# Hybrid decoder block: how the low parts of the mixers' and gates' weights are formed

## The chip, the cores and the metric

The kernel runs on one core of a Trainium2 chip. The metric is the device time of one execution in microseconds (us); the median of three runs of the kernel before is 965.05 us (963.51 to 967.03).

## The reference, cut to what matters

```python
u    = rmsnorm(h, norm1_g)
proj = u @ w_in            # split into q, k, v, z, decays (GDN), q, k, v, indexer (DSA), two gates
o_gdn = gated_delta_rule_chunked(...)   # after a causal conv of width 4 and SiLU on q, k, v
o_dsa = dsa_sparse_attention(...)       # top 128 keys by the indexer's score, then softmax
mixed = sigmoid(gate_a + ...) * o_gdn + sigmoid(gate_b + ...) * o_dsa
h = h + mixed @ w_out
h = h + (silu(gate) * val) @ ffn_w_down  # gate, val: a conv of width 3 over rmsnorm(h) @ ffn_w_up
out = rmsnorm(h)
```

The sequence has 512 tokens of 1024 channels, the gated delta net (GDN) 8 heads of 128, the sparse attention (DSA) 8 heads over 2 key and value heads, the feed-forward part 2816 channels. All of it is float32.

## The kernel before, in words

**Split products.** TensorE multiplies in a format (float32r, `R` in the code) that holds fewer bits than float32. So every large matrix product is made of three: each operand is split into a high part, the value rounded to that format, and a low part, what is left, rounded in its turn. `passes` (L198 to L204) adds high x low (L202), low x high (L203) and high x high (L204) into one accumulator in PSUM.

**Pieces.** The weights lie in DRAM as 139 pieces of 128 x 1024 values (512 KB). `load` (L184) takes three buffers from a pool, for the piece as it is (`raw`), its high part (`whi`) and its low part (`wlo`), three of each in turn, and issues the load on SyncE's queue (SP). `piece` (L192) lets ScalarE (`A`) cast `raw` into the high part (L194), and GpSimd (`P`) or VectorE (`V`) subtract that from `raw` into the low part (L195). The first three pieces, for the DSA values and the small columns, are loaded and split apart from that, in halves (`split`, L231 to L234).

**Who uses pieces.** `channel_major` (L304) takes two pieces for 256 output channels over all 512 tokens: 24 matmuls of 512 columns for each piece, into two accumulator banks. `token_major` (L292) takes two for 256 channels with tokens as rows: 48 matmuls of 256 columns for each. There are three accumulator banks of that kind (`acc`). In the order of the program:

- four pieces for the indexer's queries (L423), 12 for the first half of the GDN heads (`gdn_half(0)`), two for the DSA keys, eight for the DSA queries (L701), 12 for the second half (`gdn_half(1)`): all by `channel_major`;
- 24 for z and the two gates by `token_major` (`z_chunk`, `ga_chunk`, `gb_chunk`);
- then 8 for the output projection (L842), 44 for the FFN's up projection (L914) and 22 for the down projection (L961), each with its `piece` call.

In the first 62, GpSimd makes the low parts, but for six in `gdn_half(1)`, where VectorE makes that of the second piece of each pair. After them VectorE makes them, but for the first four of the up projection, which GpSimd makes.

**What runs beside.** For each GDN half, the accumulators go through a causal conv (`conv_silu`, taps on VectorE at L460), heads are transposed for their norms (L488, squares on ScalarE at L490), decays are masked by GpSimd (`affine_select`, L524) and exponentiated by ScalarE, GpSimd scales the queries (L542), and a triangular system is solved on blocks of 32: the blocks go to DRAM and come back (L568, L572), VectorE eliminates column by column (a product at L583, a subtraction at L585, 30 times), and the results go the same way back (L587, L589). These transfers are issued on ScalarE's queue. The indexer's top 128 of each row are found by VectorE (L688, L689). The attention (L705 to L732) is computed in items of a head and 128 queries: VectorE adds the mask and takes the maximum, ScalarE takes the exponential (L716), TensorE transposes (L724) and multiplies (L728).

**What sets the order.** The program is written in sequence, and a scheduler interleaves it when it is built: it plans the times of all instructions on a model and lays down a fixed order for each engine. Each engine then runs its own list in order and waits on semaphores; a transfer is issued by the engine whose queue it is on, in the order of that engine's list. The tile pool adds the waits for a buffer's last users.

```python
    def piece(lo_engine):
        raw, hi, lo = load()
        A.copy(hi, raw)
        lo_engine.tensor_sub(lo, raw, hi.bitcast(F))
        return hi, lo
```

Of the kernel before, what the change touches and what calls it, by code (L numbers as in the profile page):

```python
# [9 lines left out]
F = mybir.dt.float32  # L10
R = mybir.dt.float32r
I32 = mybir.dt.int32
AF = mybir.ActivationFunctionType
OP = mybir.AluOpType
# [72 lines left out]
def hybrid_block(ctx: ExitStack, tc: tile.TileContext, x: bass.AP, xc: bass.AP, wp: bass.AP,  # L87
                 chan: bass.AP, rows: bass.AP, out: bass.AP):
    nc = tc.nc
    V, A, P, T = nc.vector, nc.scalar, nc.gpsimd, nc.tensor  # L90
# [5 lines left out]
    def acc(name="acc"):  # L96
        return psum.tile([128, 512], F, name=name, tag="acc", bufs=3)

    def tp(name="tp"):
        return psum.tile([128, 512], F, name=name, tag="tp", bufs=2)  # L100
# [4 lines left out]
    def rec(name="rec"):  # L105
        return psum.tile([128, 512], F, name=name, tag="rec", bufs=2)
# [73 lines left out]
    pipe = ctx.enter_context(tc.tile_pool(name="pipe", bufs=1))  # L180
    pipe.tile([128, 16], F, name="pad1")
    pos = [0]

    def load():  # L184
        raw = pipe.tile([128, 1024], F, name="raw", bufs=3)
        nc.sync.dma_start(raw, wp[pos[0]])
        pos[0] += 1
        hi = pipe.tile([128, 1024], R, name="whi", bufs=3)
        lo = pipe.tile([128, 1024], R, name="wlo", bufs=3)
        return raw, hi, lo  # L190

    def piece(lo_engine):  # L192
        raw, hi, lo = load()
        A.copy(hi, raw)  # L194
        lo_engine.tensor_sub(lo, raw, hi.bitcast(F))  # L195
        return hi, lo

    def passes(o, lhs, rhs, first, last, shared=False):  # L198


        (lh, ll), (rh, rl) = lhs, rhs
        a = T.matmul(o, lh, rl, start=first, stop=False, skip_group_check=shared)  # L202
        T.matmul(o, ll, rh, start=False, stop=False, skip_group_check=shared)  # L203
        return a, T.matmul(o, lh, rh, start=False, stop=last, skip_group_check=shared)  # L204

    def cols(pc, k, n, c0, c1):
        return tuple(w.rearrange("p (k c) -> p k c", c=n)[:, k, c0:c1] for w in pc)
# [12 lines left out]
    xg = [tuple(sl.tile([128, S], R, name=n, bufs=KT) for n in ("xgh", "xgl")) for _ in range(KT)]  # L220
# [68 lines left out]
    def u_blk(k, tb):  # L289
        return uTh[:, k, 128 * tb:128 * tb + 128], uTl[:, k, 128 * tb:128 * tb + 128]  # L290

    def token_major(eng):  # L292

        pcs = [piece(eng), piece(eng)]
        ps = [acc().rearrange("p (t c) -> p t c", c=256) for _ in range(2)]
        for i in range(2):
            for tb in range(NT):
                for k in range(4):
                    kk = 4 * i + k
                    passes(ps[tb // 2][:, tb % 2], u_blk(kk, tb), cols(pcs[i], k, 256, 0, 256),  # L300
                           kk == 0 and tb % 2 == 0, kk == KT - 1, shared=True)
        return ps

    def channel_major(eng, src=None, second=P):  # L304
        pcs = [piece(eng), piece(second)]
        ps = [acc(), acc()]
        for i, pc in enumerate(pcs):
            for t in range(2):
                for k in range(4):
                    kk = 4 * i + k  # L310
                    passes(ps[t], cols(pc, k, 256, 128 * t, 128 * t + 128),
                           src[kk] if src else (uTh[:, kk], uTl[:, kk]), kk == 0, kk == KT - 1)
        return ps
# [4 lines left out]
    def half_kb(name):  # L318
        return PR.tile([128, 512], F, name=name, tag="dqo", bufs=9)
# [100 lines left out]

    iq = []
    for j in range(2):
        for t, p in enumerate(channel_major(P, xg)):  # L423
            iqf = PR.tile([128, 512], F, name="iqf", tag="t", bufs=5)
            V.tensor_mul(iqf, p, rB)  # L425
            for s in range(2):
                q = PR.tile([128, 512], R, name="iq", tag="dqo", bufs=9)
                src = iqf[64 * s:64 * s + 64]
                A.copy(q[0:64], src)
                V.tensor_sub(q[64:128], src, q[0:64].bitcast(F))  # L430
                iq.append(q)
# [6 lines left out]
    for b in range(1, NT):  # L438
        n = 128 * (b + 1)
        score[b] = mask[:, m_off[b]:m_off[b] + n]  # L440
        for h in range(H):
            p = tp("rel")[:, :n]
            T.matmul(p, iq[h][:, 128 * b:128 * b + 128], ikh[:, :n], start=True, stop=False)
            T.matmul(p, iq[h][:, 128 * b:128 * b + 128], ikl[:, :n], start=False, stop=True)
            w = iw[:, b, h:h + 1]
# [23 lines left out]
    def gdn_half(hh):  # L469
# [23 lines left out]


        for j in range(2):
            for t, p in enumerate(channel_major(P, second=V if hh else P)):
                conv_silu(p, 8 + HH * hh + 2 * j + t, kT[:, 2 * j + t])
        sumsq(kT, ssk, kt)
        V.tensor_scalar(ssk, ssk, EPS, None, op0=OP.add)
# [7 lines left out]
        V.tensor_mul(kd, rk, kde[:, :, hs])  # L507

        for j in range(2):
            for t, p in enumerate(channel_major(P, second=V if hh else P)):  # L510
                conv_silu(p, HH * hh + 2 * j + t, qT[:, 2 * j + t])
        sumsq(qT, ssq, None)
        V.tensor_scalar(ssq, ssq, EPS, None, op0=OP.add)
# [5 lines left out]
        for c in range(NT):  # L519
# [10 lines left out]
            for h2 in range(2):  # L530
                p = rec("kk").rearrange("p (h a i) -> p h a i", h=2, a=2)
# [13 lines left out]


        for j in range(2):
            for t, p in enumerate(channel_major(P, second=V if hh else P)):
                h = 2 * j + t
                vT = conv_silu(p, 16 + HH * hh + h)  # L550
                pv = rec("vt").rearrange("p (c d) -> p c d", d=128)
                for c in range(NT):
                    T.transpose(pv[:, c], vT[:, 128 * c:128 * c + 128], ident)
                for c in range(NT):
                    A.activation(vt[:, c, h], pv[:, c], AF.Identity, scale=nk[:, c, h:h + 1])
# [24 lines left out]
        for j in range(1, 31):  # L580
            m, c = 31 - j, (j + 1) // 2
            w = tw[:, :c * m].rearrange("p (r i) -> p r i", i=m)
# [93 lines left out]
        oA.append(at)  # L676

    gdn_half(0)


# [10 lines left out]


    dk = PR.tile([128, 2, 512], F, name="dk", tag="k4", bufs=2)
    for t, p in enumerate(channel_major(P)):
        A.copy(dk[:, t], p)
    dq = []
    for j in range(4):
        for t, p in enumerate(channel_major(P)):
            q = half_kb("dq")
            A.copy(q, p)  # L700
            dq.append(q)  # L701

    gdn_half(1)

    oB = []  # L705
# [60 lines left out]
        V.scalar_tensor_tensor(o, t, 1.0, o, op0=OP.add, op1=OP.mult)  # L766

    def z_chunk(j):
        for t2, p in enumerate(token_major(P)):
            t = tmp("tz")  # L770
            A.activation(t, p, AF.Tanh, scale=0.5)
            V.scalar_tensor_tensor(t, t, 1.0, p, op0=OP.add, op1=OP.mult)
            o = oAv[j][:, 2 * t2:2 * t2 + 2]
            P.tensor_mul(o, o, t)

    def ga_chunk(j):
        bias = gate_bias(256 * j)
        for t2, p in enumerate(token_major(P)):
            gated(oAv[j][:, 2 * t2:2 * t2 + 2], p, bias)

    def gb_chunk(j):
        bias = gate_bias(1024 + 256 * j)
        for t2, p in enumerate(token_major(P)):
            tb = slice(2 * t2, 2 * t2 + 2)
            t = tmp("tg")
            V.tensor_add(t, p, bias)
            A.activation(t, t, AF.Tanh, scale=0.5)
            for i in range(2):
                o = oB[2 * j + i][:, tb]
                V.scalar_tensor_tensor(o, t[:, :, 128 * i:128 * i + 128], 1.0, o, op0=OP.add, op1=OP.mult)  # L790
# [50 lines left out]
    for j in range(4):  # L841
        pcs = [piece(V), piece(V)]  # L842
# [70 lines left out]
    for f in range(NF):  # L913
        e = P if f < 2 else V  # L914
        pcs = [piece(e), piece(e)]
# [123 lines left out]
```

## Time and profile before

| what | value |
|---|---|
| median of three runs | 965.05 us |
| the profiled execution | 965.41 us |
| its span, first to last instruction | 963.4 us |
| mean granted TensorE clock | 0.990 |
| TensorE busy | 923.5 us |
| VectorE busy | 615.2 us |
| ScalarE busy | 439.7 us |
| GpSimd busy | 205.3 us |
| read from HBM | 85.18 MB |

The profile is of one execution; its span leaves out about 2 us around the first and the last instruction. Engines stand in it as PE (TensorE; PEld is its loading of weights), DVE (VectorE), ACT (ScalarE), POOL (GpSimd) and SP (SyncE); a q behind the name is the engine's queue of issues. Issuing a transfer is not counted as busy time. A line such as L195 is the kernel's. A group is written as what is written <- what is read, with the shape, the count, the busy time and the mean of one, then the idle time of the engine before these instructions and what ended it. PEclk is the granted clock, 1.00 for 2.4 GHz; the DMA share is that of the 16 engines' time. Matmuls are pipelined, so that the busy time of TensorE counts their overlap once.

### The profile page before, as it was taken

Reading aid. Unit: us, or ns where it says so; the run is one execution under the profiler, and the core shown is the slowest. Engines: PE = TensorE matmul, PEld = TensorE weight load, DVE = VectorE, ACT = ScalarE, POOL = GpSimd, SP = SyncE. Lnnn points to the kernel's source line nnn. Section 1 sums busy time; section 2 is a strip of 40 time slices with the busy share of each in tenths; the row PEclk is TensorE's granted clock in tenths of the full one; section 3 lists DMA queues with packets and bytes.
Section 4 is the critical chain, followed back from the end, with each engine's and each line's share of the span. In section 5 each row is a group of like instructions: output and inputs, shape, how many; then the busy total and the mean of one; then the engine's idle time right before and its main releaser. Section 6 shows DMA issues by size and latency. Waiting matters only on the chain.

```text
span 963.4 us, 14652 instructions
## 1 busy us (share of the span) xinstructions
PE 923.5 (96%) x5671; PEld 806.4 (84%) x5671; DVE 615.2 (64%) x1262; ACT 439.7 (46%) x938; POOL 205.3 (21%) x120
## 2 busy tenths in 40 slices
PE   8889998989999898899999999999999999999997
PEld 8768887767787797899999999888888888888886
DVE  5997999897638948755543637556655666522424
ACT  7436673422458653345544436444444444421313
POOL 2744343520211254211154022100000000000201
PEclk9999999998999999999999999999999999999999
DMA  8222222324310122311322223323232332323212
GB/s 322 93 87 88 88 72 83 100 65 110 111 45 25 64 77 85 98 55 50 137 72 91 85 90 97 100 87 102 96 104 94 88 110 87 110 90 107 88 66 87
DMA packets 39541, 89.29 MB, mean 93 GB/s; under 512 B 15632, under 2 KB 16944, under 8 KB 39472
## 3 DMA queue, kind: packets, MB, share of 16 engines
q1 hardware_dynamic: 24048, 82.05, 26.0%
q10 hardware_dynamic: 15424, 6.31, 2.7%
q8 instruction: 44, 0.72, 0.3%
q14 instruction: 25, 0.20, 0.1%
HBM read 85.18 MB, written 3.16 MB: 92 GB/s over the span
## 4 chain that ended last, share of the span: by engine, by line
PE 66%; DVE 22%; DMA 5%; ACT 3%; issue 2%; POOL 1%; ACTq 0%; SPq 0%; DVEq 0%; POOLq 0%
PE acc L202 17%; PE acc L204 17%; PE acc L203 17%; PE d L202 3%; PE d L203 3%; PE d L204 3%; DVE y L460 3%; DVE wi L585 2%; DVE mask L689 2%; DVE tw L583 2%; DVE top L688 2%; PE lg L728 1%; PE lg L710 1%; DMA ge<-gdr 1%; DMA nn<-bl 1%
## 5 line engine op out<-in xcount | busy, mean ns | idle before, releaser
L194 ACT CAST whi<-raw 128x1024 fp32r<-128x1024 f32 x136 | 142.3, 1047 | 175.7 <-PE acc L204 77.0
L195 POOL TENSOR_TENSOR wlo<-raw,whi 128x1024 fp32r<-128x1024 f32 x60 | 147.5, 2460 | 295.4 <-ACT whi L194 248.2
L195 DVE TENSOR_TENSOR wlo<-raw,whi 128x1024 fp32r<-128x1024 f32 x76 | 94.3, 1241 | 147.5 <-ACT whi L194 147.4
L203 PE MATMUL acc<-hTh,wlo 128*128 128x512 f32 (+1 forms) x368 | 139.8, 380 | 0.0
L202 PE MATMUL acc<-hTl,whi 128*128 128x512 f32 (+1 forms) x368 | 139.1, 381 | 0.2 <-DVE hTl L837 0.2
L204 PE MATMUL acc<-hTh,whi 128*128 128x512 f32 (+1 forms) x368 | 138.8, 380 | 0.0
L202 PE MATMUL acc<-uTl,whi 128*128 128x512 f32 x272 | 109.1, 402 | 5.3 <-DVE iqf L425 4.3
L203 PE MATMUL acc<-uTh,wlo 128*128 128x512 f32 x272 | 108.9, 400 | 5.1 <-DVE wlo L195 5.1
L204 PE MATMUL acc<-whi,uTh 128*128 128x256 f32 x384 | 113.3, 295 | 0.0
L202 PE MATMUL acc<-wlo,uTh 128*128 128x256 f32 x384 | 112.2, 292 | 0.0
L203 PE MATMUL acc<-whi,uTl 128*128 128x256 f32 x384 | 112.1, 292 | 0.0
L204 PE MATMUL acc<-uTh,whi 128*128 128x512 f32 x272 | 108.9, 400 | 0.0
L979 POOL TENSOR_TENSOR h<-h,gf 128x512 f32<-128x512 f32 (+1 forms) x8 | 10.6, 1344 | 338.6 <-ACT sq L975 338.6
L896 DVE SCALAR_TENSOR_TENSOR fy<-acc,ch,fy 128x511 f32<-128x511 f32 x88 | 65.8, 748 | 26.2 <-ACT fy L894 24.7
L202 PEld LDWEIGHTS acc<-hTl,whi 128*128 128x128 f32 x368 | 69.2, 188 | 13.5 <-DVE hTl L837 0.4
L204 PEld LDWEIGHTS acc<-hTh,whi 128*128 128x128 f32 x368 | 69.2, 188 | 13.1
L203 PEld LDWEIGHTS acc<-hTh,wlo 128*128 128x128 f32 x368 | 69.2, 188 | 13.1
L202 PEld LDWEIGHTS acc<-wlo,uTh 128*128 128x128 f32 x384 | 73.9, 193 | 1.6 <-issue 1.0
L204 PEld LDWEIGHTS acc<-whi,uTh 128*128 128x128 f32 x384 | 73.8, 192 | 1.7 <-issue 1.0
L203 PEld LDWEIGHTS acc<-whi,uTl 128*128 128x128 f32 x384 | 74.0, 193 | 1.2 <-issue 1.0
L202 PEld LDWEIGHTS acc<-uTl,whi 128*128 128x128 f32 x272 | 52.1, 192 | 16.6 <-DVE iqf L425 4.8
L203 PEld LDWEIGHTS acc<-uTh,wlo 128*128 128x128 f32 x272 | 52.1, 191 | 15.5 <-DVE wlo L195 5.5
(313 smaller groups left out, 1916.9 us busy)
## 6 DMA issues: line engine op xcount, KB each, us to landing
raw<-in_wp_dram SPq DMA_DIRECT2D x139, 512.0 KB, 3.4
xT<-in_xc_dram SPq DMA_DIRECT2D x8, 256.0 KB, 6.0
xt<-in_x_dram SPq DMA_DIRECT2D x4, 512.0 KB, 7.8
ge<-gdr ACTq DMA_DIRECT2D x8, 256.0 KB, 3.4
h<-in_x_dram SPq DMA_DIRECT2D x4, 512.0 KB, 6.0
out_dram<-h SPq DMA_DIRECT2D x8, 256.0 KB, 2.2
gbias<-in_rows_dram ACTq DMA_DIRECT2D x8, 128.0 KB, 3.1
nn<-bl ACTq DMA_DIRECT2D x4, 256.0 KB, 4.8
```

Source lines behind the costliest of these rows:

```text
L194: A.copy(hi, raw)
L195: lo_engine.tensor_sub(lo, raw, hi.bitcast(F))
L202: a = T.matmul(o, lh, rl, start=first, stop=False, skip_group_check=shared)
L203: T.matmul(o, ll, rh, start=False, stop=False, skip_group_check=shared)
L204: return a, T.matmul(o, lh, rh, start=False, stop=last, skip_group_check=shared)
L460: V.scalar_tensor_tensor(y[:, s:], p[:, :512 - s], cw[:, ti, 3 - s:4 - s], y[:, s:], op0=OP.mult, op1=OP.add)
L583: V.tensor_mul(w, wi[:, 0:c, j:j + 1].to_broadcast([128, c, m]), nn[:, j:j + 1, j + 1:].to_broadcast([128, c, m]))
L585: V.tensor_sub(wi[:, 0:c, j + 1:], wi[:, 0:c, j + 1:], w)
L688: V.max(top, score[b])
L689: V.match_replace(score[b], top, score[b], TAKEN)
L896: V.scalar_tensor_tensor(y[:, s:], p[:, :512 - s], fw[:, ti, 2 - s:3 - s], y[:, s:], op0=OP.mult, op1=OP.add)
L979: P.tensor_mul(hv, hv, gf[:, 512 * half + c.start:512 * half + c.stop])
```

## The change

In `piece`, a call that names no engine now does the following: ScalarE writes the negated piece, rounded, into the low part's buffer; a transfer issued by GpSimd then reads the piece from DRAM a second time and adds it to what stands there; ScalarE casts the high part after that. All calls from `channel_major` and `token_major` (62 pieces) name none, so GpSimd subtracts nothing there, and neither does VectorE in the second half. The output projection and the FFN call as before. For all pieces there are two buffers for `raw` instead of three, and four for `wlo` instead of three. Cut to one call of each kind:

```diff
     def load():
-        raw = pipe.tile([128, 1024], F, name="raw", bufs=3)
+        raw = pipe.tile([128, 1024], F, name="raw", bufs=2)
         nc.sync.dma_start(raw, wp[pos[0]])
         pos[0] += 1
         hi = pipe.tile([128, 1024], R, name="whi", bufs=3)
-        lo = pipe.tile([128, 1024], R, name="wlo", bufs=3)
+        lo = pipe.tile([128, 1024], R, name="wlo", bufs=4)
         return raw, hi, lo
 
-    def piece(lo_engine):
+    def piece(lo_engine=None):
+        w = wp[pos[0]]
         raw, hi, lo = load()
-        A.copy(hi, raw)
-        lo_engine.tensor_sub(lo, raw, hi.bitcast(F))
+        if lo_engine is None:
+            A.activation(lo, raw, AF.Copy, scale=-1.0)
+            P.dma_start(lo, w, accum_op=OP.add)
+            A.copy(hi, raw)
+        else:
+            A.copy(hi, raw)
+            lo_engine.tensor_sub(lo, raw, hi.bitcast(F))
         return hi, lo
...
-    def token_major(eng):
+    def token_major():
-        pcs = [piece(eng), piece(eng)]
+        pcs = [piece(), piece()]
...
-    def channel_major(eng, src=None, second=P):
-        pcs = [piece(eng), piece(second)]
+    def channel_major(src=None):
+        pcs = [piece(), piece()]
...
-            for t, p in enumerate(channel_major(P, second=V if hh else P)):
+            for t, p in enumerate(channel_major()):
```

## Rows read from the trace of the kernel before

**Rows 1.** The head of the page: the span, and each engine's busy time.

```profile
span 963.4 us, 14652 instructions
PE 923.5 (96%) x5671; PEld 806.4 (84%) x5671; DVE 615.2 (64%) x1262; ACT 439.7 (46%) x938; POOL 205.3 (21%) x120
```

**Rows 2.** Ten stages of the span, busy times in us, columns above them.

```profile
core 0: us, PE busy (x) PEld busy (x) DVE busy (x) ACT busy (x) POOL busy (x), PEclk, DMA share, GB/s
0.00:25.00 25.00, 21.96 (x146) 20.77 (x147) 13.74 (x36) 18.63 (x32) 6.85 (x14) 1.00 0.85 315
25.00:55.00 30.00, 27.42 (x120) 22.27 (x118) 29.21 (x41) 12.66 (x20) 20.20 (x10) 0.94 0.27 88
55.00:65.00 10.00, 5.41 (x18) 3.90 (x16) 9.72 (x34) 4.17 (x7) 3.75 (x2) 0.83 0.17 52
65.00:150.00 85.00, 84.87 (x413) 71.08 (x414) 77.50 (x173) 54.27 (x152) 33.06 (x17) 1.00 0.27 88
150.00:212.00 62.00, 58.73 (x281) 47.75 (x280) 58.70 (x143) 24.06 (x48) 28.18 (x17) 1.00 0.31 90
212.00:232.00 20.00, 14.48 (x50) 11.03 (x49) 15.03 (x46) 1.74 (x2) 0.00 (x0) 0.83 0.39 99
232.00:310.00 78.00, 74.06 (x594) 62.06 (x595) 49.56 (x99) 46.99 (x130) 11.97 (x7) 1.00 0.19 57
310.00:420.00 110.00, 99.92 (x896) 92.50 (x895) 82.80 (x228) 54.47 (x163) 39.66 (x24) 0.98 0.27 78
420.00:600.00 180.00, 179.98 (x1503) 176.37 (x1502) 96.81 (x229) 86.89 (x207) 48.65 (x23) 1.00 0.27 88
600.00:963.00 363.00, 356.68 (x1663) 298.75 (x1661) 182.17 (x238) 135.85 (x183) 12.99 (x9) 1.00 0.29 95
```

**Rows 3.** What TensorE waited for: us in total, times, longest us.

```profile
PE pT L724 <- ACT pe L716: 5.6, 4, 2.4
PE acc L203 <- DVE wlo L195: 5.1, 1, 5.1
PE acc L202 <- DVE iqf L425: 4.3, 1, 4.3
```

**Rows 4.** Page, line groups: low and high parts' casts and subtractions.

```profile
L195 POOL TENSOR_TENSOR wlo<-raw,whi 128x1024 fp32r<-128x1024 f32 x60 | 147.5, 2460 | 295.4 <-ACT whi L194 248.2
L194 ACT CAST whi<-raw 128x1024 fp32r<-128x1024 f32 x136 | 142.3, 1047 | 175.7 <-PE acc L204 77.0
```

**Rows 5.** Timeline of VectorE: start us, us, engine line, operation, tiles.

```profile
54.16 2.25 DVE L389 TENSOR_TENSOR gd<-gd,s 128x32 f32<-128x32 f32 x1
...
209.21 2.34 DVE L583 TENSOR_TENSOR tw<-wi,nn 128x105 f32<-128x105 f32 x1
...
211.88 0.28 DVE L583 TENSOR_TENSOR tw<-wi,nn 128x120 f32<-128x120 f32 x1
...
216.25 1.22 DVE L195 TENSOR_TENSOR wlo<-raw,whi 128x1024 fp32r<-128x1024 f32 x1
...
226.63 2.32 DVE L460 SCALAR_TENSOR_TENSOR y<-acc,cw,y 128x511 f32<-128x511 f32 x3 [0.51 <-ACT y L458]
...
380.41 2.47 DVE L585 TENSOR_TENSOR wi<-wi,tw 128x120 f32<-128x120 f32 x1
```

**Rows 6.** Timeline of GpSimd, 205 to 222 us, same columns.

```profile
208.43 2.99 POOL L195 TENSOR_TENSOR wlo<-raw,whi 128x1024 fp32r<-128x1024 f32 x1 [8.48 <-ACT whi L194]
```

**Rows 7.** Timeline of ScalarE and its queue, 196 to 240 us, same columns.

```profile
201.43 1.05 ACT L194 CAST whi<-raw 128x1024 fp32r<-128x1024 f32 x1 [3.95 <-issue]
...
224.56 1.30 ACTq L587 DMA_DIRECT2D bl<-wi  x2
```

**Rows 8.** DMA issues: tiles, queue, count, KB each, us to landing.

```profile
raw<-in_wp_dram SPq DMA_DIRECT2D x139, 512.0 KB, 3.4
...
nn<-bl ACTq DMA_DIRECT2D x4, 256.0 KB, 4.8
```

**Rows 9.** Line group of ScalarE's casts between 150 and 420 us.

```profile
L194 ACT CAST whi<-raw 128x1024 fp32r<-128x1024 f32 x31 | 32.5, 1047 | 25.9 <-issue 5.3 <-PE vt L553 4.9 <-POOL wlo L195 4.0
```

More of the change, by code (lines that the diff above doesn't have):

```diff
@@ L422, in hybrid_block @@
     for j in range(2):
-        for t, p in enumerate(channel_major(P, xg)):
+        for t, p in enumerate(channel_major(xg)):
             iqf = PR.tile([128, 512], F, name="iqf", tag="t", bufs=5)
@@ L509, in gdn_half @@
         for j in range(2):
-            for t, p in enumerate(channel_major(P, second=V if hh else P)):
+            for t, p in enumerate(channel_major()):
                 conv_silu(p, HH * hh + 2 * j + t, qT[:, 2 * j + t])
@@ L547, in gdn_half @@
         for j in range(2):
-            for t, p in enumerate(channel_major(P, second=V if hh else P)):
+            for t, p in enumerate(channel_major()):
                 h = 2 * j + t
@@ L693, in hybrid_block @@
     dk = PR.tile([128, 2, 512], F, name="dk", tag="k4", bufs=2)
-    for t, p in enumerate(channel_major(P)):
+    for t, p in enumerate(channel_major()):
         A.copy(dk[:, t], p)
@@ L697, in hybrid_block @@
     for j in range(4):
-        for t, p in enumerate(channel_major(P)):
+        for t, p in enumerate(channel_major()):
             q = half_kb("dq")
@@ L768, in z_chunk @@
     def z_chunk(j):
-        for t2, p in enumerate(token_major(P)):
+        for t2, p in enumerate(token_major()):
             t = tmp("tz")
@@ L777, in ga_chunk @@
         bias = gate_bias(256 * j)
-        for t2, p in enumerate(token_major(P)):
+        for t2, p in enumerate(token_major()):
             gated(oAv[j][:, 2 * t2:2 * t2 + 2], p, bias)
@@ L782, in gb_chunk @@
         bias = gate_bias(1024 + 256 * j)
-        for t2, p in enumerate(token_major(P)):
+        for t2, p in enumerate(token_major()):
             tb = slice(2 * t2, 2 * t2 + 2)
```

## The prediction

> **What bounds the kernel now.** I read the head of the page first, then the span by stages, what TensorE waits for, and last the timelines of the other engines in the stages where TensorE idles. TensorE is busy for 923.5 of 963.4 us [rows 1]: whatever the change does elsewhere, it can gain only out of the 40 us in which TensorE idles, and a little where its clock was held down. The stages say where those are [rows 2]. From 65 to 150 us and from 420 to 600 TensorE has no gap; after 600 the change touches only the number of buffers. What is left: 2.6 us idle in 25 to 55, 4.6 in 55 to 65, 3.3 in 150 to 212, 5.5 in 212 to 232, 3.9 in 232 to 310 and 10.1 in 310 to 420. In 55 to 65 and in 212 to 232 the granted clock is 0.83 besides, part of the time at 1.2 instead of 2.4 GHz after the idle time: 0.17 x 10 = 1.7 and 0.17 x 20 = 3.4 us more.
>
> In those stages VectorE is the late one: busy 29.2 of 30 us, then 9.7 of 10, then 58.7 of 62 [rows 2]. Two of the three longest waits of TensorE are on it: 5.1 us for a low part that VectorE itself writes, 4.3 us for an emptied accumulator (iqf) [rows 3]. And VectorE is late in part because of GpSimd. While GpSimd's subtraction ran from 208.43 to 211.42 [rows 6], a VectorE product of 105 columns took 2.34 us; the next one of its line, larger at 120 columns, took 0.28 [rows 5]. So a VectorE instruction stands until the subtraction is through. In the first half's triangular solve there are five such (at 181.77, 189.29, 192.51, 197.90 and 209.21 us, 1.6 to 2.2 us too long each, some 9.6 together; the last stands in the rows), in the second half three (near 373.7, 380.4 and 388.3, some 2 each; the middle one stands), and three between 37 and 57 us (7 together; 54.16 is the last) [rows 5].
>
> **What goes.** 56 of GpSimd's 60 subtractions at 2.46 us [rows 4], 138 us of GpSimd, and six of VectorE's at 1.22 [rows 5]. GpSimd's own time is on no path; the VectorE time that it held is. By stage, as share of TensorE's idle and slow-clock time: in 55 to 65, 5 of 6.3 us come back, since VectorE is 7 us earlier and TensorE's 4.3 us wait for it ends. In 25 to 55 nothing: the same relief is there, but the first low part now comes by a transfer instead of a 2.46 us subtraction, and TensorE waits for that. In 150 to 212, 1 us of 3.3. In 212 to 232, 6 of 8.9: the high part that TensorE needs was ready at 202.48 [rows 7], its low part stood in VectorE's order behind the solve until 216.25 [rows 5]; that wait of 5.1 us is gone. Late next are the accumulators: the conv taps that empty them stand behind the solve at 226.63 [rows 5], and with 9.6 + 1.2 us less ahead of them they come about when TensorE wants the banks. In 232 to 310, 1 us. In 310 to 420, 3 of 10.1: VectorE's solve there is 6 us shorter, but TensorE's longest wait is on ScalarE (5.6 us) [rows 3]. Sum: 5 + 1 + 6 + 1 + 3 = 16 us.
>
> **What comes on ScalarE.** 62 negating passes over 128x1024; the cast of that shape takes 1.05 us [rows 4], so 65 us. From 65 to 150 and 420 to 600 ScalarE has room (54.3 of 85, 86.9 of 180) and TensorE's queue of pieces covers it. In 310 to 420 the exponentials that TensorE waits for share ScalarE with some twelve passes; if a quarter of them stand in that chain, 12 x 1.05 / 4 = 3 us. Without cover, all of them: 12.6 us.
>
> **What comes as transfers.** 62 accumulating ones of 512 KB, issued by GpSimd behind the wait for ScalarE. No row shows one. Issue: between 0.65 us (an issue on ScalarE's queue, two in 1.30 [rows 7]) and 2.46, one pass of GpSimd over the data [rows 4]; I take 1, nearer the issue, as no element passes through the engine. What stands behind it on GpSimd (masks, qT, the z products) waited for 2.46 us before, so nothing gets later there. Landing: at least the plain load's 3.4 us [rows 8], at most three times that, 10.2, if the read of the source, the read of the old value and the write take turns; I take 6.8, since write and read overlap in the plain load too. The Trainium skill (Collectives: The Full Stack, "Why ReduceScatter is half of AllGather") says that an adding transfer is slower for its two source reads and not for the adding; by it the landing would be the same 6.8, as an estimate, and no run here shows it yet.
>
> Lead: a piece lasts 85 us x 88 GB/s = 7.5 MB, 14.3 pieces in 65 to 150, so 5.9 us [rows 2]. A high part waits for the buffer of three pieces back (the cast's idle time is ended by TensorE [rows 4]) and so is ready two pieces, 11.8 us, early. The low part has four buffers and may start three pieces early, 17.7 us. It needs 1.05 + 1 + 6.8 = 8.9 us, at the upper ends 1.05 + 2.46 + 10.2 = 13.7. Hidden at either end, so nothing in the steady stages.
>
> The four small transfers in each half's solve (nn<-bl, 4.8 us [rows 8], and three others) share the engines with twice the bytes: between 0 and half of 4.8 each; I take 0.4 x 8 = 3 us.
>
> **What moves.** Load buffers go from three to two. The load is now let go by ScalarE's cast, no longer by GpSimd. At the start the third load waits for the first split, about 1 us, while the 16 engines are 85% busy with what was issued before [rows 2]: nothing. After 600 us a load has 11.8 us less cast, subtraction and landing, 1.05 + 1.24 + 3.4 = 5.7: hidden; without that cover each piece could lose the difference. The order on each engine is laid down at build time from planned times; it will differ, which I can't price and put at 3 us either way.
>
> **Sum.** The profiled execution took 965.4 us (963.4 of span and 2.0 around it), 0.4 over the median of 965.05. 965.4 - 16 + 3 + 3 = 955.4; against the median, 955.0.
>
> **Rivals.** First, **the transfers set the pace** (slower). In 65 to 150 the loads hold the engines 0.27 x 85 = 23 us, 1.6 per piece [rows 2]. TensorE's 5.9 us leave 4.3 for the added one; above that point, 2.7 loads' worth, TensorE waits for every low part. At four loads' worth, 8.0 us per piece: 14 pieces lose 2.1 each, 29 us, and the 22 pieces from 150 to 310 (7.3 us each) 0.7, 15 us: 1009. For it: nothing shows the adding rate. Against: a landing would have to be four plain ones. Chance 0.12.
>
> Second, **ScalarE eats the gain**. 31 casts lie between 150 and 420 us [rows 9]; as many new passes are 32.5 us. If 0.4 of them stand in chains that TensorE waits for, 13 us, nothing is gained; at 0.6, 19.5: 965.4 - 16 + 19.5 + 3 = 972. For it: TensorE's longest wait. Against: ScalarE is busy 24.1 of 62 and 54.5 of 110 us there [rows 2]. Chance 0.16.
>
> Third, **the hold only changes its cause**: GpSimd's issue and VectorE stand in each other's way as the subtraction did. Then only the 5.1 us wait for VectorE's low part goes, against the same 6 us of costs: 966. Against it: the issue reads no tile, and the subtraction's hold lasts as long as its reads. Chance 0.14. The Trainium skill (SBUF — State Buffer, "Who interferes with whom") speaks for it in part: a transfer issued from GpSimd is held up by VectorE copies and scalar operations on SBUF; no run here shows that yet.
>
> **How the numbers follow.** My case 0.58, 944 to 962: the low end gets back 21 of the 32.5 us of idle and slow-clock time (25 to 55 left out) at no cost; the high end, half the relief. 0.3%, 3 us, is about what a measurement can tell from no change. Faster: 0.58 and 0.05 of the third. Same: 0.09 of the third, 0.04 of the second. Slower: 0.12 and 0.12. The range, 944 to 974, takes in the second and third rival and leaves out the first and a tail.
>
> **What would show it.** Right: no 2 us VectorE products in the solves but beside GpSimd's other products; no wait of TensorE for L195; 55 to 65 without idle time; the accumulating transfer landing in 5 to 9 us. Wrong: TensorE waiting for wlo's transfer in 65 to 150 (first rival), for ScalarE in 150 to 420 by over 15 us more (second), or VectorE delays at GpSimd's issues (third).

## The result and the profile after

The changed kernel takes 976.54 us (median of four runs, 972.61 to 978.63), the kernel before 964.83 beside it: ratio 1.0119, 95% interval 1.0101 to 1.0137. It is slower, by 11.7 us or 1.2%, where 955 (944 to 974) was forecast. The profiled span is 972.9 us against 963.4.

The head of the page of the changed kernel, against [rows 1]:

```profile
PE 926.2 (95%) x5671; PEld 809.2 (83%) x5671; DVE 554.3 (57%) x1256; ACT 494.3 (51%) x1000; POOL 120.8 (12%) x126
```

VectorE lost 61 us of busy time, GpSimd 84; ScalarE gained 55. TensorE is now idle for 46.7 us, before for 39.9. Summed over the whole span by the engine that ended the wait, TensorE's waits on VectorE fell from 20.9 to 13.0 us, while those on ScalarE rose from 10.9 to 21.4 and those on transfers from nothing to 3.8. So the relief that was forecast is there, and ScalarE takes more than it gave. The stages, with the columns of [rows 2] (busy us of PE, PEld, DVE, ACT, POOL, then the granted clock, the DMA share and GB/s):

```profile
25.00:55.00 30.00, 26.21 (x118) 21.05 (x117) 24.22 (x71) 20.41 (x29) 11.46 (x10) 1.00 0.94 206
55.00:65.00 10.00, 10.00 (x52) 8.31 (x50) 5.20 (x13) 6.70 (x12) 1.73 (x2) 1.00 0.80 179
65.00:150.00 85.00, 81.82 (x378) 66.24 (x377) 66.23 (x165) 63.33 (x159) 12.26 (x16) 0.98 0.67 155
150.00:212.00 62.00, 55.82 (x269) 46.01 (x268) 49.21 (x158) 28.04 (x51) 13.46 (x16) 0.94 0.69 165
212.00:232.00 20.00, 20.00 (x91) 16.59 (x90) 10.28 (x30) 8.49 (x12) 3.45 (x4) 1.00 0.82 168
232.00:310.00 78.00, 69.56 (x564) 58.56 (x563) 37.15 (x83) 45.70 (x119) 6.48 (x8) 0.93 0.44 99
310.00:420.00 110.00, 98.94 (x736) 91.97 (x734) 69.75 (x234) 70.15 (x191) 23.42 (x25) 1.00 0.63 138
420.00:600.00 180.00, 176.34 (x1602) 172.01 (x1603) 88.49 (x218) 91.09 (x204) 23.15 (x20) 0.99 0.44 116
```

The holes that the prediction meant to close are closed: 55 to 65 and 212 to 232 are full, at a clock of 1.00. Others are open in 65 to 150 and 420 to 600, which had none, and have grown in 150 to 212 (from 3.3 to 6.2 us idle) and 232 to 310 (from 3.9 to 8.4) [rows 2]. TensorE's longest waits (total us, times, longest), against [rows 3]:

```profile
PE m L609 <- DVE UT L603: 5.9, 2, 3.6
PE acc L210 <- ACT dq L708: 5.9, 2, 4.8
PE lg L718 <- ACT oB L740: 5.8, 5, 2.3
PE upd L655 <- ACT vt L650: 3.9, 1, 3.9
PE acc L211 <- DMA wlo<-in_wp_dram: 3.8, 2, 2.8
```

Three of the five are on ScalarE. What ScalarE itself waits for stands in its line groups (what the low part was costs GpSimd and VectorE [rows 4, 5]); the last line is GpSimd's issue of the adding transfer:

```profile
L198 ACT ACTIVATE wlo<-raw 128x1024 fp32r<-128x1024 f32 x62 | 65.5, 1056 | 90.2 <-DMA raw<-in_wp_dram 76.5 <-PE m L626 6.5 <-PE acc L210 3.6
L200 ACT CAST whi<-raw 128x1024 fp32r<-128x1024 f32 x62 | 64.7, 1043 | 10.4 <-PE acc L212 10.3
L199 POOL DMA_DIRECT2D wlo<-in_wp_dram x62 | 54.1, 872 | 370.0 <-ACT wlo L198 273.7 <-ACT sqj L498 43.8 <-PE acc L212 16.2
```

ScalarE stands still for 76.5 us ahead of its negations because the piece has not been loaded yet. One such place, ScalarE's timeline from 190 us (start, us, line, tiles, in brackets the idle time before and what ended it):

```profile
190.12 1.06 ACT L198 ACTIVATE wlo<-raw 128x1024 fp32r<-128x1024 f32 x1 [4.08 <-DMA raw<-in_wp_dram]
...
191.55 1.05 ACT L200 CAST whi<-raw 128x1024 fp32r<-128x1024 f32 x1
...
194.51 1.10 ACT L200 CAST whi<-raw 128x1024 fp32r<-128x1024 f32 x1
199.83 1.06 ACT L198 ACTIVATE wlo<-raw 128x1024 fp32r<-128x1024 f32 x1 [4.21 <-DMA raw<-in_wp_dram]
200.79 0.57 ACT L708 COPY dq<-acc 128x512 f32<-128x512 f32 x1
```

The chain of waits through the same place (start, us, what):

```profile
191.66 0.95 ACT whi L200
192.61 0.02 issue
192.63 7.12 DMA raw<-in_wp_dram
...
199.83 1.00 ACT wlo L198
200.83 0.53 ACT dq L708
```

And TensorE:

```profile
196.24 0.39 PE L212 MATMUL acc<-uTh,whi 128*128 128x512 f32 x1
201.41 0.79 PE L210 MATMUL acc<-uTl,whi 128*128 128x512 f32 x1 [4.79 <-ACT dq L708]
```

The high cast of 191.55 lets a load buffer go; the load that wanted it is issued at 192.63 and lands after 7.1 us, while an adding transfer that GpSimd began to issue at 191.48 is under way. The negation that reads it already stands at the head of ScalarE's list. Behind it stands the copy dq that empties an accumulator, and TensorE waits 4.8 us for that; its next product takes 0.79 us instead of 0.39, and the granted clock from 200 to 206 us is 0.50, the level of 1.2 GHz. The page puts 12% of the chain that ended last on loads of pieces.

The transfers themselves (issues, KB each, median us to landing), after, to be held against [rows 8]:

```profile
raw<-in_wp_dram SPq DMA_DIRECT2D x139, 512.0 KB, 3.7
wlo<-in_wp_dram POOLq DMA_DIRECT2D x62, 512.0 KB, 6.6
...
MT<-bl ACTq DMA_DIRECT2D x8, 64.0 KB, 6.7
```

and the last of these before:

```profile
MT<-bl ACTq DMA_DIRECT2D x8, 64.0 KB, 2.2
```

### The profile page after: what moved, and what is told of

Read it like the earlier page. It is cut to its first block, busy times and chain, and to the rows that moved or that the text cites. A ratio compares the mean times of both kernels' runs of the same rounds, so it can differ in the third digit from the quotient of the medians.

```text
span 972.9 us, 14741 instructions
## 1 busy us (share of the span) xinstructions
PE 926.2 (95%) x5671; PEld 809.2 (83%) x5671; DVE 554.3 (57%) x1256; ACT 494.3 (51%) x1000; POOL 120.8 (12%) x126
## 4 chain that ended last, share of the span: by engine, by line
PE 61%; DMA 18%; DVE 8%; ACT 8%; issue 4%; POOL 1%; ACTq 1%; SPq 0%; DVEq 0%; POOLq 0%
PE acc L211 15%; PE acc L212 15%; PE acc L210 15%; DMA raw<-in_wp_dram 12%; PE d L210 3%; PE d L211 3%; PE d L212 3%; ACT wlo L198 2%; ACT whi L200 2%; DMA wlo<-in_wp_dram 2%; DVE mask L697 2%; DMA MT<-bl 1%; DVE top L696 1%; DMA ge<-gdr 1%; PE lg L736 1%
## 5 line engine op out<-in xcount | busy, mean ns | idle before, releaser
L203 DVE TENSOR_TENSOR wlo<-raw,whi 128x1024 fp32r<-128x1024 f32 x70 | 87.1, 1244 | 141.2 <-ACT whi L202 141.2
L198 ACT ACTIVATE wlo<-raw 128x1024 fp32r<-128x1024 f32 x62 | 65.5, 1056 | 90.2 <-DMA raw<-in_wp_dram 76.5
L199 POOL DMA_DIRECT2D wlo<-in_wp_dram x62 | 54.1, 872 | 370.0 <-ACT wlo L198 273.7
L210 PEld LDWEIGHTS acc<-hTl,whi 128*128 128x128 f32 x368 | 69.2, 188 | 13.6 <-DVE hTl L845 0.4
L200 ACT CAST whi<-raw 128x1024 fp32r<-128x1024 f32 x62 | 64.7, 1043 | 10.4 <-PE acc L212 10.3
```

Of the source, the lines that this page charges most:

```text
L198: A.activation(lo, raw, AF.Copy, scale=-1.0)
L199: P.dma_start(lo, w, accum_op=OP.add)
```

## The experiments

Three theories stood at the start. A: ScalarE's ordered list waits for late loads, because two load buffers let them go late. B: the 65 us of new work on ScalarE cost as such. C: the added bytes delay loads and small transfers, whatever the buffers. Ratios are to the kernel before in the same session, with 95% intervals; where versions of different sessions are set against each other, the difference is taken from the ratios. The diffs are cut to what matters; in e1 and e2 they are given in short, where `raw` is the load's buffer and `wlo` the low part's.

**e1: three load and three low buffers, as before the change.**

```diff
-raw bufs=2, wlo bufs=4
+raw bufs=3, wlo bufs=3
```

> The changed kernel with three load buffers and three low-part buffers (the numbers of the kernel before). Theory A, ScalarE's ordered list waits for late loads because a piece has only two load buffers while a load beside an adding transfer lands after about 7 us: the waits of ScalarE's negation for the load (76.5 us in the changed kernel) fall below 30 us, the 4.8 us stall of TensorE at 196 us goes, and the time is 962 to 968 us. Theory B, ScalarE's 65 us more work as such: unchanged, 974 to 978. Theory C, the added bytes on the 16 DMA engines delay the solve's small transfers and the loads whatever the buffers: 972 to 978.

Measured: 956.07, ratio 0.9903 (0.9882 to 0.9924). With the buffers of before, the change is a gain, and of the size that the prediction forecast; it lies below the range of A too. ScalarE's negations:

```profile
L198 ACT ACTIVATE wlo<-raw 128x1024 fp32r<-128x1024 f32 x62 | 65.5, 1056 | 40.7 <-PE acc L211 36.8 <-PE acc L210 3.7
```

The wait for loads is gone, with the same 62 passes and the same bytes: B and C alone cannot carry the loss. This run changes both buffer counts, though, and I took the load buffers to be the one that matters.

**e2: the kernel before with only the buffer counts of the change.**

```diff
-raw bufs=3, wlo bufs=3
+raw bufs=2, wlo bufs=4
```

> The kernel before with only the buffer numbers of the change (two for loads, four for low parts). Theory A: with loads that land after 3.4 us two buffers are nearly enough, 964 to 969 us. If the buffers alone explain the loss, 974 to 978. Theories B and C: 964 to 966.

Measured: 962.36, ratio 0.9983 (0.9968 to 0.9997). The counts alone cost nothing; it takes the new pass.

**e3: the changed kernel, GpSimd negates.**

```diff
-A.activation(lo, raw, AF.Copy, scale=-1.0)
+P.tensor_scalar(lo, raw, -1.0, None, op0=OP.mult)
```

> The changed kernel, but GpSimd writes the negated piece instead of ScalarE (62 one-operand passes). Theory A: ScalarE no longer waits for loads at the negation, but GpSimd's transfer and the high part's cast still come after the load: 964 to 970 us. Theory B: ScalarE is back at its old load, 958 to 964. Theory C: 972 to 978, as the traffic is the same.

Measured: 959.26, ratio 0.9948 (0.9923 to 0.9973). The pass, now on GpSimd:

```profile
L198 POOL TENSOR_SCALAR wlo<-raw 128x1024 fp32r<-128x1024 f32 x62 | 175.4, 2829 | 194.8 <-DMA raw<-in_wp_dram 76.8 <-PE acc L211 63.7 <-PE acc L210 46.5
```

It waits for loads as long, 76.8 us, and yet the kernel is faster than before. That the wait hurts through what stands behind it on ScalarE fits this, though this run alone doesn't show it. The time itself lies in B's range; e1, which is faster still with the pass on ScalarE, speaks against B.

**e4 and e5: ScalarE's pass stays, the adding transfer goes, GpSimd subtracts all 62 pieces.** e4 has the buffers of the change, e5 three and three.

```diff
 A.activation(lo, raw, AF.Copy, scale=-1.0)
-P.dma_start(lo, w, accum_op=OP.add)
 A.copy(hi, raw)
+P.tensor_sub(lo, raw, hi.bitcast(F))
```

> No adding transfers: ScalarE's negating pass stays where the change has it, and GpSimd then subtracts as before and overwrites its result (all 62 on GpSimd, buffers as in the change). Theory B: 975 to 985 us, the ScalarE work plus the subtraction's hold on VectorE. Theory A: loads land after 3.4 us again, the negation seldom waits, 966 to 972. Theory C: 963 to 967.

> The run with ScalarE's negating pass and GpSimd's subtraction (no adding transfers), now with three load buffers and three low-part buffers. Theory A, a ScalarE pass is dear only where it stands in ScalarE's list waiting for a load, which two buffers cause: the negation's waits for loads (24.9 us there) nearly vanish and the time falls from 976 to 963 to 968 us. Theory B, the 65 us of ScalarE work are dear in themselves: it stays at 973 to 980.

Measured: e4 976.41, ratio 1.0114 (1.0089 to 1.0138); e5 970.3, ratio 1.0054 (1.0039 to 1.0069). With three load and three low buffers ScalarE's pass (and six low parts moved from VectorE to GpSimd) costs 5 us beside the old subtraction; the other buffers cost 6 more. e4 falls in B's range and e5 between those of A and B, so a part of B may hold, 5 us. In e4 the negation still waits 24.9 us for loads, though loads land after 3.5 us: the slow loads of the change make the wait longer, they do not make it.

```profile
L198 ACT ACTIVATE wlo<-raw 128x1024 fp32r<-128x1024 f32 x62 | 65.5, 1056 | 49.6 <-DMA raw<-in_wp_dram 24.9 <-DVE UT L601 16.2 <-DVE at L548 4.0
```

**e6: the kernel before with a memory-to-memory copy of each of the 62 pieces, issued by GpSimd.**

```diff
 raw, hi, lo = load()
+idle = dram.tile([128, 1024], F, name="idle", bufs=2)
+P.dma_start(idle, w)
```

> The kernel before plus 62 transfers that GpSimd issues, each copying the same 512 KB piece from DRAM into a DRAM tile that nobody reads. No waits for data, subtractions and buffers as before. Theory C, traffic alone lengthens the loads and the small transfers of the solve and of the decays (gdr<-gts 1.4 us, ge<-gdr 3.4 us before): loads land after 5 us or more, the small ones take twice as long, and the time is 970 to 978 us. Theory A: the same slower loads, but three buffers hide them: 964 to 969.

Measured: 1041.83, ratio 1.0798 (1.076 to 1.0836). A miss: the copies waited for no piece, ran ahead and all fell into the first 130 us, where they took 12.8 us each to land. It says nothing of traffic in its place; e10 does that.

**e7: the changed kernel with the high cast written ahead of the negation.**

```diff
+A.copy(hi, raw)
 A.activation(lo, raw, AF.Copy, scale=-1.0)
 P.dma_start(lo, w, accum_op=OP.add)
-A.copy(hi, raw)
```

> The changed kernel (two load buffers, four for low parts, adding transfers) with the high part's cast written ahead of the negation, so that the cast waits for the load and the negation never stands alone in ScalarE's list for it. Theory A: the negation's waits for the load go from 76 us to below 30, and the time falls to 955 to 966 us. Theories B and C: 973 to 979, since work and traffic are the same.

Measured: 977.57, ratio 1.0124 (1.0094 to 1.0154). The negation still waits 87.9 us for loads:

```profile
L199 ACT ACTIVATE wlo<-raw 128x1024 fp32r<-128x1024 f32 x62 | 65.6, 1058 | 99.3 <-DMA raw<-in_wp_dram 87.9 <-PE m L626 6.3 <-PE acc L210 4.7
```

The order in the source is not the order on the engine: the scheduler still put the negation of the next piece ahead of this piece's high cast in 40 of 61 cases. The edit didn't do what it was meant to.

**e8: from e1, but the 16 pieces up to the first half of the gated part are subtracted by GpSimd as before; adding transfers for the other 46.**

```diff
-channel_major(xg)
+channel_major(xg, P)
...
-channel_major()
+channel_major(eng=None if hh else P)
```

> Adding transfers only from the DSA keys on (46 pieces); the indexer's and the first GDN half's 16 pieces are subtracted by GpSimd as before; three buffers of each kind. With three buffers everywhere the version with 62 adding transfers was 9 us behind the kernel before at 140 us and made up 19 us after that. If the loss comes from the adding transfers of that first stretch, where the decays' small transfers and 16 pieces come close together, this gives 944 to 952 us; if the order of the whole list matters more, 954 to 962.

Measured: 948.9, ratio 0.9829 (0.9813 to 0.9846), faster than both kernels. In e1 TensorE had fallen 10.7 us behind by piece 16 and made up 21 after that; e8 has nearly none of the first (0.8 us behind at piece 16).

**e9: the changed kernel with three low buffers, load buffers still two.**

```diff
-lo = pipe.tile([128, 1024], R, name="wlo", bufs=4)
+lo = pipe.tile([128, 1024], R, name="wlo", bufs=3)
```

> The changed kernel with three buffers of the low part in place of four, the load buffers left at two. Theory A (the negation waits in ScalarE's list for a load that its two buffers let go late): no gain, 973 to 981, the negation's wait for loads still over 60 us. If instead the fourth low buffer did the harm, by letting adding transfers run ahead and lengthen loads: 956 to 964 as with three of each.

Measured: 952.11, ratio 0.9881 (0.9854 to 0.9907). Theory A falls as I had put it: two load buffers alone do not bring the loss. It went with the fourth low buffer, to a time below both ranges. (Three load and four low buffers were not run, so whether the harm needs two load buffers besides is open.)

```profile
L198 ACT ACTIVATE wlo<-raw 128x1024 fp32r<-128x1024 f32 x62 | 65.5, 1057 | 39.0 <-PE acc L211 30.1 <-DMA raw<-in_wp_dram 5.0 <-PE acc L210 3.6
```

The loads of these 62 pieces are as slow here (6.6 us from issue to landing in the median) as in the changed kernel (6.3), and yet the negation waits for them 5.0 us and not 76.5. What differs is ScalarE's order. In the changed kernel the negation of piece n+1 stands ahead of the high cast of piece n in 39 of 61 cases, in e7 in 40 and in e4, without adding transfers, in 24; in e1, e5 and e9 in none. That cast lets the buffer for the load of piece n+2 go. With a fourth low buffer the planner can start a negation one piece earlier, does so, and the cast, which must wait for TensorE to let a high buffer go, comes behind; the load of n+2 then starts a step late, and its negation is again the next thing but one in the list. With three low buffers, as many as high ones, both passes of a piece wait for products of the same earlier piece, and they stand side by side. That this is why the planner chose so is argued from the two orders; what the order costs is tested in e13.

**e10: traffic in its place.** The kernel before, a copy behind each of GpSimd's 56 subtractions.

```diff
-lo_engine.tensor_sub(lo, raw, hi.bitcast(F))
+sub = lo_engine.tensor_sub(lo, raw, hi.bitcast(F))
+if more and lo_engine is P:
+    idle = dram.tile([128, 1024], F, name="idle", bufs=2)
+    after(P.dma_start(idle, w), sub)
```

> The kernel before (three buffers of each kind) with one more transfer per piece: a copy of the piece, memory to memory, issued by GpSimd right behind its subtraction, for the 56 pieces that GpSimd subtracts; nobody waits for it. Theory C (added bytes delay loads and small transfers whatever the buffers): 973 to 985, some 10 to 20 us more than before. Theory A (a longer load is covered as long as a third buffer stands ready): 962 to 970, within 5 us of before, though loads beside a copy land later than 3.4 us.

Measured: 971.91, ratio 1.0083 (1.0054 to 1.0113): 8 us, between the two expectations. The copies cost something though nobody waits for them. How much of it is their bytes is open: issuing them also keeps GpSimd busy for 30 us, and the planner laid the other instructions in another order too. The short transfers of the solve land later in it:

```profile
idle<-in_wp_dram POOLq DMA_DIRECT2D x56, 512.0 KB, 5.0
...
nn<-bl ACTq DMA_DIRECT2D x4, 256.0 KB, 6.2
...
MT<-bl ACTq DMA_DIRECT2D x8, 64.0 KB, 5.6
```

nn<-bl took 4.8 before [rows 8], MT<-bl 2.2. So C may hold in part, but 8 us are below the 21 to 30 between the changed kernel and its versions with another order (e1, e9, e13), which move the same bytes. A copy also writes to DRAM (32.5 MB written in e10, 3.2 before), which the adding transfers don't (3.2 after).

**e11 and e12: GpSimd negates in e1 and in e8** (the edit of e3).

> The changed kernel with three load and three low buffers, and GpSimd writes minus the piece in place of ScalarE. Theory A with what is left of B (ScalarE's pass as such costs some 5 us): 948 to 954, below the 956 with ScalarE's pass. If ScalarE's pass cost nothing beyond the wait for loads, or GpSimd's longer pass lengthens the lead of the low part: 955 to 960, and TensorE's waits for the low part over 13 us.

> The version that subtracts on GpSimd up to the middle of the gated part and adds from there on (948.9 with ScalarE's pass), with GpSimd writing minus the piece. If ScalarE's pass still costs behind 420 us: 944 to 948. If TensorE there is covered either way: 948 to 950, the same within 0.3%.

Measured: e11 963.48, ratio 0.9987 (0.9974 to 1.0001); e12 969.65, ratio 1.0054 (1.0036 to 1.0071). Both miss: GpSimd's pass is the worse one once the order is right, by 8 and by 22 us. In e11 the first low part of the 62 pieces is used 5.6 us later than in e1, and there is one wait of 10.3 us for a low part; why e12 loses as much as it does was not followed.

**e13: the changed kernel with one order laid down.** This tells apart O (the fourth low buffer does harm through ScalarE's order alone) and F (it does harm by itself, by letting adding transfers run ahead).

```diff
-A.activation(lo, raw, AF.Copy, scale=-1.0)
+neg = A.activation(lo, raw, AF.Copy, scale=-1.0)
+if last:
+    after(neg, last[0])
 P.dma_start(lo, w, accum_op=OP.add)
-A.copy(hi, raw)
+last[:] = [A.copy(hi, raw)]
```

> The changed kernel as it is, two load and four low buffers, with one order laid down: each negation stands on ScalarE behind the previous piece's high cast. Theory O (the fourth low buffer does harm only because it lets the next negation stand in ScalarE's list ahead of the high cast that lets its successor's load go, so that the list waits for loads): 948 to 959, the negation's wait for loads under 10 us in place of 76.5. Rival F (the fourth buffer does harm by itself: adding transfers start earlier and lengthen loads and small transfers): 970 to 979.

Measured: 944.73 (944.04 to 948.61), ratio 0.9812 (0.9783 to 0.984). With two load and four low buffers and every transfer of the change, the kernel is 30 us faster by the ratios (1.0119 against 0.9812), more than theory O had expected. F falls. With e8, whose interval overlaps, it is the fastest version. Its negations and high casts (L199 and L203 in it):

```profile
L199 ACT ACTIVATE wlo<-raw 128x1024 fp32r<-128x1024 f32 x62 | 65.8, 1061 | 2.7 <-DMA raw<-in_wp_dram 2.6
L203 ACT CAST whi<-raw 128x1024 fp32r<-128x1024 f32 x62 | 65.0, 1049 | 19.4 <-PE acc L215 19.1
```

76.5 us of waiting for loads have become 2.6. (Its loads also land sooner, after 4.1 us in the median for the 62 pieces, but that is not needed for it: in e9 they take 6.6 and the negation waits 5.0 us.) ScalarE's timeline, in the same part of the kernel as the one shown above:

```profile
186.01 0.59 ACT L711 COPY dq<-acc 128x512 f32<-128x512 f32 x1 [2.13 <-PE acc L215]
186.49 1.05 ACT L203 CAST whi<-raw 128x1024 fp32r<-128x1024 f32 x1
187.44 1.06 ACT L199 ACTIVATE wlo<-raw 128x1024 fp32r<-128x1024 f32 x1
191.51 1.06 ACT L203 CAST whi<-raw 128x1024 fp32r<-128x1024 f32 x1 [3.00 <-PE acc L215]
192.47 1.05 ACT L199 ACTIVATE wlo<-raw 128x1024 fp32r<-128x1024 f32 x1
194.17 0.59 ACT L711 COPY dq<-acc 128x512 f32<-128x512 f32 x1 [0.65 <-PE acc L215]
```

Each cast is followed by the next piece's negation, whose load has landed; here ScalarE waits for TensorE and not the other way round. Over the whole span TensorE's waits on ScalarE are 1.7 us, where they were 21.4 in the changed kernel and 10.9 before. Its longest waits:

```profile
PE m L612 <- DVE UT L606: 6.3, 2, 4.2
PE acc L214 <- DMA wlo<-in_wp_dram: 2.8, 1, 2.8
...
PE lg L721 <- ACT oB L743: 1.6, 2, 1.3
```

TensorE in it (columns as above):

```profile
65.00:150.00 85.00, 85.00 (x408) 70.92 (x407) 73.77 (x187) 67.61 (x164) 14.37 (x18) 1.00 0.77 168
150.00:212.00 62.00, 62.00 (x307) 52.23 (x306) 50.42 (x161) 31.78 (x55) 14.00 (x17) 1.00 0.86 187
```

The chain that ended last is TensorE's for 81% in e13:

```profile
PE 81%; DVE 8%; DMA 7%; ACT 2%; issue 1%; ACTq 0%; POOL 0%; SPq 0%; DVEq 0%
```

In the changed kernel it was for 61%, and transfers had 18% in place of 7:

```profile
PE 61%; DMA 18%; DVE 8%; ACT 8%; issue 4%; POOL 1%; ACTq 1%; SPq 0%; DVEq 0%; POOLq 0%
```

How far this shows the cause: the edit lays down one order, but the planner then moves others too. Of ScalarE's 796 instructions that are neither negations nor high casts, 86 stand elsewhere in the list than in the changed kernel, of VectorE's 1256, 184 (counted from the traces, against the longest order that both share). So the 30 us are the price of the plan with the inversion, and not of the inversion alone. For the inversion speaks that e1, e9 and e13 have none and lose nothing, though the rest of the lists differs as much between e9 and e13 (109 and 209 instructions); that e7, which keeps it in 40 cases, loses as much as the changed kernel; and that what goes is TensorE's waiting for ScalarE. The rest of the plan is worth some 7 us, by which e9 and e13 differ with no inversion in either.

**e14 and e15: e8 with two load buffers; e8 with two load and four low buffers and the order of e13.**

> The version that subtracts on GpSimd up to the middle of the gated part and adds from there on, with two load and three low buffers (three and three gave 948.9). Theory O: load buffers are no matter as long as negation and high cast of a piece stand side by side: 944 to 951. If two load buffers cost where GpSimd subtracts at the start: 951 to 956.

> The same version with two load and four low buffers and the negation ordered behind the previous piece's high cast. Theory O: within 4 us of the one with three low buffers, 944 to 955. Rival F: 955 to 970.

Measured: e14 948.98, ratio 0.9855 (0.9826 to 0.9885); e15 954.31, ratio 0.9899 (0.9876 to 0.9921). e14 equals e8: with three low buffers the load buffers are no matter. e15 misses its "within 4 us" by a little: its order is the one of e13, its negation waits 3.5 us for loads, and yet it is some 4 us slower than e14 by the ratios; why was not followed. Subtracting at the start gains nothing over e13, where the start is no longer late.

How far TensorE is, as the start of its first product with the low part of the n-th of the 62 pieces (counted from 0), in us against the same product before (worked out from the start times in the four traces; minus is earlier). Work other than these products can stand ahead of a piece in one kernel and behind it in another, so single columns swing by some us for that alone:

```
piece              6      18      27      36      48     end
after           -5.4     0.0    +0.3    +7.5    -0.5    +9.4
e9 (lo=3)       -2.7    +7.9    -2.1    -2.2   -24.2   -12.9
e13 (order)     -5.2    -6.0   -15.2   -12.6   -26.0   -20.5
```

## Why the prediction was wrong

**The failed step is the order on the engines,** "it will differ, which I can't price and put at 3 us either way". Plans of the same work lie some 30 us apart (ratio 1.0119 against 0.9812 in e13), and the term could have been bounded. Two terms next to it were read the wrong way. "The low part has four buffers and may start three pieces early, 17.7 us ... Hidden at either end" counted the fourth buffer as lead. What it did was to let the negation go into ScalarE's list ahead of the cast on which the load after it depends; 29 of the 62 negations began within 0.15 us of their load's landing, so they had no lead to speak of. And "the load is now let go by ScalarE's cast" was followed up at the start and after 600 us only, where it is harmless, and not in the 62 pieces, where ScalarE now also reads the load first. On the trace that cost 76.5 us of ScalarE waiting for loads, and TensorE waited 21.4 us for ScalarE where it had waited 10.9. The question what is queued behind a waiting instruction was put to GpSimd's queue and not to ScalarE's.

**VectorE's relief: right, and larger than counted.** VectorE products no longer stand for GpSimd. The 120 products and subtractions of the two solves take 30.5 us in place of 43.4, the longest 1.13 us where 2.47 stood [rows 5]. (Two of the five delays that the prediction put into the first solve are not its products: the one at 181.77 is on the indexer's mask, the one at 189.29 writes the block from which the solve starts, wi<-nn.) In all, VectorE's busy time fell by 61 us, of which the six low parts are 7; the prediction counted 23 of the other 54. While GpSimd issued an adding transfer, VectorE worked on; the two timelines of the changed kernel (GpSimd, then VectorE), against the 2.34 us of [rows 5, 6]:

```profile
202.61 0.86 POOL L199 DMA_DIRECT2D wlo<-in_wp_dram  x1 [0.57 <-ACT wlo L198]
```

```profile
202.85 0.22 DVE L591 TENSOR_TENSOR tw<-wi,nn 128x75 f32<-128x75 f32 x1
```

This also ends the third rival: of the 137 VectorE instructions that ran beside an issue of an adding transfer, 136 took as long as others of their kind, within 0.02 us. The rule of the Trainium skill that was put on its side (SBUF — State Buffer, "Who interferes with whom") is about an issue that waits while VectorE copies or does scalar operations on SBUF, and not while it multiplies two tensors as above. It may show a little: the 62 issues took 0.87 us in the mean, and the two longest, 1.02 us at 23.27 and 0.98 at 379.52, each ran beside a scalar operation of VectorE that reads and writes SBUF (0.29 and 0.42 us); all others took 0.90 us or less. That is 0.15 us at the most.

**Stages.** 55 to 65: TensorE full and 5.3 us ahead at piece 5, as forecast (5). 212 to 232: the wait of 5.1 us for VectorE's low part is gone. What is late there next is not the accumulators, as the prediction had it: in e13 TensorE's longest wait, 4.2 us, is for the solve's result (m<-UT above), and the stage is 15.8 of 20 us busy. In e13, where the order does not hide the relief, TensorE gains 7 us between pieces 18 and 36, about 150 to 308 us (forecast 1 + 6 + 1), and 8 more from there to the end, where the forecast had 3 gained in 310 to 420 and 3 lost to ScalarE. That stage was the mis-sized term in the relief: -20.5 at the end of e13 against the forecast's -10. ScalarE's new passes cost TensorE nothing there: its waits on ScalarE after 310 us are 1.4 us in e13, 8.3 before.

**ScalarE.** The second rival gave 972, near the measured time, but not by its mechanism: e13 has the same 65 us of passes and is 18 us faster than the kernel before. TensorE's waits on ScalarE did rise, from 10.9 us to 21.4, but between 150 and 420 us by 8.4 (10.9 to 19.3), under the 15 that the prediction had named as this rival's sign. With the inversion gone they are 1.7 us in e13 and 4.6 in e9: they are largely waits for loads handed on.

**Transfers.** Issue: 0.87 us, forecast 1. Landing: 6.6 us, forecast 6.8. By the page of the Trainium skill that was named there (Collectives: The Full Stack, "Why ReduceScatter is half of AllGather") two reads make an adding transfer slow; 6.6 beside 3.4 us for a plain load [rows 8] agrees with the size, though both are times beside other transfers (the shortest adding transfer took 5.3 us) and no run takes the reads from the adding. "The transfers set the pace" was rightly given little: TensorE waits 3.8 us in all for low parts that transfers bring (13.6 in e1, of which 5.7 between 65 and 150 us, and 2.8 in e13). What was missed is that plain loads beside an adding transfer can land later, 6.3 us in the median for the 62 pieces against 3.4, as the load was taken at 3.4 throughout; how much later hangs on the order too, 4.1 us in e13. The small transfers were put at 3 us; e10 gives 8 us for all effects of such copies in the kernel before.

**The sign and the range.** The case for faster held in its mechanism and lost to the term that was put at 3 us without a reason. The range reached to 974 for the second and third rival; the measured 976.54 lies just above it, by a mechanism that no rival names. A rival for it could have been worked out: 31 casts stand between 150 and 420 us [rows 9], so about as many negations; had a third of them waited for a load of 3.4 us [rows 8], that alone would have been 35 us of ScalarE, more than the whole relief of 16. That is an estimate; how much of it TensorE would have waited for can't be read from those rows.

## What to carry to other kernels

An instruction that gets another buffer may also get another place in its engine's list, ahead of the very instruction that lets its successor's input go; then the list waits for a transfer, and everything behind it does too. When a pass that reads a load moves to an engine on which the critical path depends, write down for two pieces in a row which instruction lets which load start and in which order they stand, and fix that order by hand where the planner is free. Buffer counts should be tried one at a time: here two changed together, and the one that looked dangerous, two load buffers in place of three, did no harm with three low buffers (e9, e14) or with the order laid down (e13). When an edit changes what the planner sees, the rest of its plan changes as well, so count what else moved before giving the whole difference to the edit.

## What the runs showed of the hardware

- Beside adding transfers of the same size, a 512 KB load that takes 3.4 us took 6.3 in the median in the changed kernel and 6.6 in e9, but 4.1 in e13, where it ran beside them as well (57 of the 62 for over half of their time). A 64 KB transfer (MT<-bl) went from 2.2 to 6.7 us.
- An adding transfer of 512 KB lands after 6.4 to 7.1 us in the median (changed kernel, e1, e9, e13), never under 5.2.
- A VectorE subtraction of 128x120 beside a GpSimd subtraction took 2.47 us [rows 5]; with GpSimd's subtractions gone, no instruction of the two solves takes over 1.13.
- GpSimd's one-operand negation of 128x1024 takes 2.83 us, longer than its two-operand subtraction of that shape (2.46 [rows 4]).
- GpSimd issues an adding transfer in 0.87 us; the issue of a plain copy in e10 took 0.54:

```profile
L199 POOL DMA_DIRECT2D idle<-in_wp_dram x56 | 30.1, 538 | 0.0
```
